# Two groups of pre-added weights, loaded at two moments instead of one

## The chip, the cores and the metric

The kernel runs on one core of a Trainium2 chip. The metric is the device time of one execution in microseconds (us). Three runs of the kernel before took 1237.09, 1238.32 and 1242.99 us; the median, 1238.32, is the time before.

## What is computed

The reference is a decoder trunk of two layers over 256 positions of width 1024, in float32:

```python
for l in range(DEPTH):                                   # DEPTH = 2
    x = x + 0.5 * swiglu_ffn(rms_norm(x, ffn1_norm[l]), ffn1_w_in[l], ffn1_w_out[l])
    h = rms_norm(x, mix_norm[l])
    uv, c_q, c_kv, k_rope, z, xbc, dt_raw, gates = split(h @ w_in[l])
    y_a, y_b, y_c = gmlp(uv), attention(c_q, c_kv, k_rope), ssd(z, xbc, dt_raw)
    g = sigmoid(gates)
    x = x + (sum_i g_i * (y_i @ w_branch[l, i])) @ w_out[l]
    x = x + 0.5 * swiglu_ffn(rms_norm(x, ffn2_norm[l]), ffn2_w_in[l], ffn2_w_out[l])

def swiglu_ffn(h, w_in, w_out):                          # w_in: 1024 x 5632, w_out: 2816 x 1024
    gate, up = split(h @ w_in, 2)
    return (silu(gate) * up) @ w_out
```

The change touches only the first product of `swiglu_ffn`, `h @ w_in`. It runs four times: FFN (0,0) and (0,1) in the first layer, (1,0) and (1,1) in the second, with the mixing part between the two of a layer.

## The kernel before

**Precision.** Each float32 matrix is cut into a high part (`whi`, a cast on ScalarE, L177) and a rest (`wlo`, a subtraction on VectorE, L178), and each product is three TensorE matmuls (L223 to L225): high x high, high x low, low x high.

**Weights.** All weights lie in one long array in the order of use, cut into chunks of 512 KB (128 x 1024). `load` (L147) brings a chunk into one of five `raw` buffers on SyncE's DMA queue; a load waits until the chunk five places earlier has been split. `split` cuts it into one of four pairs of `whi` and `wlo`, up to four chunks ahead of TensorE (`AHEAD = 3`, L130, L209).

**Narrow chunks.** 14 of the 22 blocks of 128 features come in seven narrow groups of four chunks. A narrow chunk is 12 matmuls, which fill `ps_in`.

**Wide groups.** The other 8 blocks come in two wide groups, j = 0 and 1. Each is a product of 2 x 2 blocks done with seven block products instead of eight, as in Winograd's form of Strassen's scheme. `b11`, `b22` and `b21` use blocks of the weight as they are; `t1` to `t4` use sums of blocks. Each of the seven steps is two chunks of six matmuls, as long in all as one narrow chunk. The results go to `ps_wa` (`wide["A"]`), `ps_wd` (`wide["D"]`) and `ps_we`. `wide["m"]` is a copy of A after b11 (L444); `wide["v"]` is a copy of A after t3, with D added.

**The sums.** t1's weight is b11 + b12 and t3's is b22 + b12. They are made by DMAs of the POOL (GpSimd) queue, in `load_sums` (L153): a plain load of the base chunk (L168), and on top of it an accumulating load of the b12 chunk (L171), which waits for the first. So each of t1 and t3 takes four transfers of 512 KB per group: two chunks, each loaded and then added to. The other sums are made on VectorE in place: t2 = t3 + b11 (L200; b11's chunk is loaded again for it), t4 = t2 + b21 (L195). In the code, b21's chunk is split and then added at L195.

**When the sums are loaded.** The first group's eight transfers are issued before the FFN starts, or in (0,0) once the norm's factors exist. The second group's eight are issued in program order after the step b22 of the first group. A DMA without a dependency may be moved up as far as its buffer is free. To hold t1's sums back, a POOL copy of one column from `wide["v"]` into their buffer stands ahead of them (`behind`, L165). t3's sums of both groups share one buffer (tag `xbc`) and have no copy for the second group; they start when the first group's t3 chunks have been read. t1's sums of the second group lie in a buffer of their own (tag `big12b`).

**Order.** The order of the chunks is `_ffn_order` (L55): `lead` narrow chunks, then the seven steps of group 0 with `gaps[0]` narrow chunks behind each, then group 1 with `gaps[1]`. Behind step b11 stands the place of b12, which takes no step. `aside`, the loads of the tables and of the mixing part's parameters, is called at entry 12 of the order in (0,0). The instruction order on each engine is then made by the Tile framework's planner, which runs the program through a timeline of its own; `split` is given high priority. Within an engine the instructions run in that order.

Of the kernel before, what the change touches and what calls it, by code (L numbers as in the profile page):

```python
# [10 lines left out]
F32 = mybir.dt.float32  # L11
# [4 lines left out]
ALU = mybir.AluOpType  # L16
# [3 lines left out]
P = 128  # L20
# [34 lines left out]
def _ffn_order(key):  # L55

    narrow = [("n", g, c) for g in range(NARROW) for c in range(4)]
    if key == (0, 0):
        lead, gaps = 12, [[2, 1, 1, 1, 1, 1, 1]] * 2
    else:  # L60
        lead, gaps = 4, [[2] * 7, [2, 1, 1, 2, 1, 1, 2]]
    order, narrow = narrow[:lead], narrow[lead:]
    for j in range(WIDE):
        for names, n in zip((("b11", "b12"), ("t1",), ("t2",), ("t3",), ("b22",), ("b21",), ("t4",)), gaps[j]):
            order += [(name, j, c) for name in names for c in range(2)]
            order += narrow[:n]
            narrow = narrow[n:]
    assert not narrow
    return order
# [36 lines left out]
SUB_MAX = 1024  # L106
# [4 lines left out]
def tile_trunk(ctx, tc, wst, xtok, xT, pos, pcol, prow, wsT, cst, out):  # L111
    nc = tc.nc
    act, dve, pool, pe = nc.scalar, nc.vector, nc.gpsimd, nc.tensor
# [3 lines left out]
    bp = ctx.enter_context(tc.tile_pool(name="bp", bufs=1))  # L117
# [5 lines left out]
    widths, units, chunk_at = _plan()  # L123
# [12 lines left out]
    def source(i):  # L136
        return wst[starts[i] : starts[i] + P * widths[i]].rearrange("(p n) -> p n", p=P)
# [12 lines left out]

    sums = {}

    def load_sums(key, j, behind=None):  # L153

        if j == 0:
            xs = [bp.tile([P, SUB_MAX], F32, name="xsum", tag=t) for t in ("vg", "zt")]
            sums[key, "y"] = bp.tile([P, 2, SUB_MAX], F32, name="ysum", tag="xbc")
        else:
            both = bp.tile([P, 2, SUB_MAX], F32, name="xsum", tag="big12b")
            xs = [both[:, c] for c in range(2)]  # L160
        for c in range(2):
            sums[key, "t1", j, c], sums[key, "t3", j, c] = xs[c], sums[key, "y"][:, c]
            if behind is not None:
                for t in (xs[c], sums[key, "y"][:, c])[: 2 - j]:
                    pool.tensor_copy(t[:, 0:1], behind)  # L165
        for name, base in (("t1", "b11"), ("t3", "b22")):
            for c in range(2):
                pool.dma_start(out=sums[key, name, j, c], in_=source(chunk_at[key, (base, j, c)]))  # L168
        for name in ("t1", "t3"):
            for c in range(2):  # L170
                pool.dma_start(out=sums[key, name, j, c], in_=source(chunk_at[key, ("b12", j, c)]), accum_op=ALU.add)  # L171

    def parts_of(r, cuts):
        hi = wp.tile([P, SUB_MAX], F32R, name="whi", tag="whi", bufs=4)
# [226 lines left out]
    def ffn(key, nrm, nxt, last, late, aside=None):  # L401
# [28 lines left out]
        def product(ps, xs, first):  # L430

            for c in range(2):
                hi, lo = next_sub()
                for i in range(2):
                    k, w = 2 * c + i, slice(512 * i, 512 * (i + 1))
                    xhi, xlo = xs(k)
                    mm3x(ps, xhi, xlo, hi[:, w], lo[:, w], first and k == 0, k == 3, again=not first)

        xs = {}
        wide = {}  # L440
# [12 lines left out]
        def wide_step(kind, j):  # L453
            if kind == "b11":
                wide["A"] = acc.tile([P, 512], F32, name="ps_wa", tag="acc")
                product(wide["A"], plain(0, 0), True)
                wide["m"] = snap("m1", "ss")
            elif kind == "t1":
                wide["D"] = acc.tile([P, 512], F32, name="ps_wd", tag="acc")
                product(wide["D"], summed(xs[0]), True)  # L460
            elif kind == "t2":
                product(wide["A"], summed(xs[2]), False)
                wide["u"] = snap("u2", "xp")
            elif kind == "t3":
                product(wide["A"], summed(xs[1]), False)
                wide["v"] = snap("u3", "xp")
                dve.tensor_tensor(wide["v"], wide["v"], wide["D"], ALU.add)
            elif kind == "b22":
                product(wide["D"], summed(xs[3]), False)
                dve.tensor_tensor(wide["u"], wide["u"], wide["D"], ALU.add)  # L470
            elif kind == "b21":
                e = mxp.tile([P, 512], F32, name="ps_we", tag="mx")
                product(e, plain(1, 0), True)
                dve.tensor_tensor(wide["m"], wide["m"], e, ALU.add)
                gated("a0", wide["m"], 0, wide["u"])
            else:
                product(wide["A"], plain(1, 1), False)
                gated("a1", wide["A"], 1, wide["v"])
                for n in range(2):
                    s = slice(256 * n, 256 * (n + 1))  # L480
                    turns.append((2 * NARROW + 4 * j + 2 * n, [wide["u"][:, s], wide["v"][:, s]]))

        ps = None
        for n, (kind, g, c) in enumerate(_ffn_order(key)):
            if n == 12 and aside:
                aside()
            if kind != "n":
                if kind != "b12" and c == 0:
                    wide_step(kind, g)
                    if kind == "b22" and g == 0:  # L490
                        load_sums(key, 1, wide["v"][:, 0:1])
                continue
            if c == 0:
                home, tag = (acc, "acc") if g % 2 == 0 else (mxp, "mx")
                ps = [home.tile([P, 512], F32, name="ps_in", tag=tag) for _ in range(2)]
            hi, lo = next_sub()
            for i in range(2):
                k, w = 2 * c + i, slice(512 * i, 512 * (i + 1))
                for b in range(2):
                    s = halves(b)  # L500
                    mm3x(ps[b], hl[:, k, 0, s], hl[:, k, 1, s], hi[:, w], lo[:, w], k == 0, k == KD - 1)
            if n < ready:
                late[n]()
            if n == ready - 1:
                nrm.finish()
                if key == (0, 0):
                    load_sums(key, 0, nrm.rc[:, 0:1])
                big = bp.tile([P, 3, 2, 4, P], F32R, name="xs", tag="big12a")
                spots = [(big[:, m, 0], big[:, m, 1]) for m in range(3)]
                spots.append([tp.tile([P, 4, P], F32R, name="xs", tag="prob") for _ in range(2)])  # L510
            elif n in (combine, combine + 1):
                for m in (0, 1) if n == combine else (2, 3):
                    xs[m] = combined(nrm, m, *spots[m])
            turn_all()
            if c == 3:
                aa = []
                for b in range(2):
                    rcb = nrm.rc[:, b : b + 1]
                    s = tp.tile([P, 256], F32, name="s", tag="s")
                    act.activation(s, ps[b][:, 0:256], AF.Silu, scale=rcb)  # L520
                    a = at[:, g % 2, b]
                    dve.scalar_tensor_tensor(a, ps[b][:, 256:512], rcb, s, ALU.mult, ALU.mult)
                    aa.append(a)
                turns.append((2 * g, aa))
        ahl = [parts[f // 12][:, f % 12] if parts[f // 12] is not None else None for f in range(KF)]

        for h in range(2):
            hs = slice(HD * h, HD * (h + 1))
            ps = [acc.tile([P, HD], F32, name="ps_out", tag="acc") for _ in range(2)]
            f = 0  # L530
            for c in range(KF // 2):
                hi, lo = next_sub()
                for i in range(2):
                    w = slice(512 * i, 512 * (i + 1))
                    for b in range(2):
                        s = halves(b)
                        mm3x(ps[b], ahl[f][:, 0, s], ahl[f][:, 1, s], hi[:, w], lo[:, w], f == 0, f == KF - 1)
                    f += 1
                if h == 0 and c == 0:
                    turn_all()  # L540
                if h == 1 and c == 0 and not last:
                    nxt.add(0)
                if h == 1 and c == 4 and key[1] == 1 and not last:
                    load_sums((key[0] + 1, 0), 0, None)
            for b in range(2):
                dve.scalar_tensor_tensor(x[:, b, hs], ps[b], FFN_RESID, x[:, b, hs], ALU.mult, ALU.add)
                if last:
                    nc.scalar.dma_start(out=out[:, b, hs], in_=x[:, b, hs])
# [576 lines left out]
    nrm = Norm(pc[:, 0, 0:8], "big24b")  # L1125
# [10 lines left out]
    for l in range(DEPTH):  # L1136
# [9 lines left out]
        nrm, nxt = nxt, Norm(pc[:, l, 16:24], "big24a")  # L1146
        late = mix(l, nrm, nxt, late, *params)
        nrm = nxt
# [3 lines left out]
        nrm = nxt  # L1152
# [117 lines left out]
```

## Time and profile before

| | |
|---|---|
| median of three runs | 1238.32 us |
| the profiled execution, its own time | 1240.04 us |
| its span, first to last instruction | 1238.2 us |
| TensorE (PE) busy | 1214.8 us, 98% |
| VectorE (DVE) busy | 897.2 us, 72% |
| ScalarE (ACT) busy | 736.0 us, 59% |
| GpSimd (POOL) busy | 113.6 us, 9% |
| mean granted TensorE clock | 0.996 |
| moved by DMA | 254.12 MB, mean 205 GB/s |

Line numbers (L178) are those of the kernel before. A row of the timeline gives the start in us, the duration, the engine and line, the operation with output and inputs, how many, and in brackets how long the engine was idle before it and what ended that. A row of the windows gives a stretch, its length, the busy time and the number of instructions of PE, PEld (weight load), DVE, ACT and POOL, then the granted clock, the DMA engines' mean busy share, and GB/s.

### The profile page before, as it was taken

The page shows a single profiled execution, that of the slowest core. Times are in us where ns is not written, and L with a number is a line of the kernel's source. Part 1 is how long each engine was busy: PE and PEld are TensorE (multiplying, and loading weights), DVE is VectorE, ACT ScalarE, POOL GpSimd, SP SyncE. Part 2 cuts the span into 40 slices and gives each one's busy share as a digit, 9 for nine tenths or more (in the row PEclk, how much of TensorE's full clock was granted, in tenths as well). Part 3 has the DMA queues.
Part 4 walks back from the last instruction along what each step waited for, and adds up shares of the span by engine and source line. Part 5 has one row for each costly group of instructions (what it writes and reads, how often), then busy time and mean ns, then how long its engine had stood idle before and what let it go on. Part 6 is the DMA issues. An engine that isn't in the chain of part 4 may idle for free.

```text
span 1238.2 us, 16875 instructions
## 1 busy us (share of the span) xinstructions
PE 1214.8 (98%) x6252; PEld 1024.2 (83%) x6252; DVE 897.2 (72%) x1249; ACT 736.0 (59%) x1009; POOL 113.6 (9%) x130
## 2 busy tenths in 40 slices
PE   9999999999999999999999999999998999999998
PEld 7887889999788877888887888899987887878886
DVE  6787756898757786885587885578795676877853
ACT  8565545756675475664575664457556755756632
POOL 3020000031300001000001000002131000010000
PEclk9999999999999999999999999999999999999999
DMA  9995554634547668976559755545454577596662
GB/s 345 288 294 199 188 187 157 208 125 171 181 152 229 213 204 260 325 245 214 187 165 275 249 192 191 189 151 188 128 160 145 180 227 235 183 270 219 226 192 72
DMA packets 72162, 254.12 MB, mean 205 GB/s; under 512 B 8080, under 2 KB 9360, under 8 KB 72080
## 3 DMA queue, kind: packets, MB, share of 16 engines
q1 hardware_dynamic: 61856, 218.29, 51.9%
q0 software_dynamic: 9216, 33.56, 11.0%
q10 hardware_dynamic: 1008, 1.20, 0.3%
q8 instruction: 49, 0.80, 0.3%
q14 instruction: 33, 0.27, 0.1%
HBM read 251.96 MB, written 1.05 MB: 204 GB/s over the span
## 4 chain that ended last, share of the span: by engine, by line
PE 83%; DMA 5%; DVE 5%; POOL 2%; issue 2%; ACT 2%; SPq 0%; DVEq 0%; ACTq 0%
PE ps_out L223 8%; PE ps_out L224 8%; PE ps_out L225 8%; PE ps_in L224 7%; PE ps_in L225 7%; PE ps_in L223 7%; DMA raw<-in_w 5%; PE ps_in L217 3%; PE ps_in L218 3%; PE ps_in L219 3%; DVE wlo L178 3%; PE ps_g L225 2%; PE ps_g L224 2%; PE ps_g L223 2%; PE ps_br L225 2%; PE ps_wa L224 2%
## 5 line engine op out<-in xcount | busy, mean ns | idle before, releaser
L178 DVE TENSOR_TENSOR wlo<-raw,whi 128x1024 fp32r<-128x1024 f32 (+3 forms) x401 | 483.6, 1210 | 215.0 <-ACT whi L177 212.7
L177 ACT CAST whi<-raw 128x1024 fp32r<-128x1024 f32 (+3 forms) x401 | 415.6, 1039 | 347.4 <-PE ps_out L225 131.3
L224 PE MATMUL ps_in<-wlo,xg 128*128 128x512 f32 x448 | 176.2, 394 | 7.8 <-DVE wlo L178 7.8
L225 PE MATMUL ps_in<-whi,xg 128*128 128x512 f32 x448 | 173.9, 394 | 0.1
L223 PE MATMUL ps_in<-whi,xg 128*128 128x512 f32 x448 | 163.8, 398 | 1.2 <-ACT xg L331 1.2
L224 PEld LDWEIGHTS ps_in<-wlo,xg 128*128 128x128 f32 x448 | 84.4, 188 | 27.4 <-DVE wlo L178 9.9
L225 PEld LDWEIGHTS ps_in<-whi,xg 128*128 128x128 f32 x448 | 83.9, 189 | 17.3 <-DVE xg L332 0.5
L223 PEld LDWEIGHTS ps_in<-whi,xg 128*128 128x128 f32 x448 | 83.0, 189 | 17.9 <-ACT xg L331 1.6
L218 PE MATMUL ps_in<-xg,whi 128*128 128x256 f32 x336 | 95.4, 286 | 0.0
L219 PE MATMUL ps_in<-xg,wlo 128*128 128x256 f32 x336 | 94.5, 283 | 0.0
L217 PE MATMUL ps_in<-xg,whi 128*128 128x256 f32 x336 | 94.5, 287 | 0.0
L224 PE MATMUL ps_g<-wlo,xg 128*128 128x512 f32 x192 | 76.7, 400 | 0.0
L225 PE MATMUL ps_g<-whi,xg 128*128 128x512 f32 x192 | 76.7, 399 | 0.0
L224 PE MATMUL ps_out<-wlo,aa 128*128 128x512 f32 x192 | 75.8, 395 | 0.0
L225 PE MATMUL ps_out<-whi,aa 128*128 128x512 f32 x192 | 75.4, 393 | 0.0
L223 PE MATMUL ps_out<-whi,aa 128*128 128x512 f32 x192 | 75.1, 392 | 0.0
L223 PE MATMUL ps_g<-whi,xg 128*128 128x512 f32 x192 | 74.5, 398 | 0.0
L219 PEld LDWEIGHTS ps_in<-xg,wlo 128*128 128x128 f32 x336 | 64.0, 191 | 0.3
L218 PEld LDWEIGHTS ps_in<-xg,whi 128*128 128x128 f32 x336 | 64.0, 191 | 0.1
L217 PEld LDWEIGHTS ps_in<-xg,whi 128*128 128x128 f32 x336 | 63.1, 190 | 1.0 <-issue 0.7
L224 PE MATMUL ps_out<-wlo,ab 128*128 128x512 f32 x160 | 62.2, 389 | 0.0
L223 PE MATMUL ps_out<-whi,ab 128*128 128x512 f32 x160 | 62.2, 389 | 0.0
(328 smaller groups left out, 2362.9 us busy)
## 6 DMA issues: line engine op xcount, KB each, us to landing
raw<-in_w SPq DMA_DIRECT2D x397, 512.0 KB, 4.2
xsum<-in_w POOLq DMA_DIRECT2D x32, 512.0 KB, 8.7
ysum<-in_w POOLq DMA_DIRECT2D x32, 512.0 KB, 8.4
raw<-in_w SPq DMA_DIRECT2D x8, 414.0 KB, 3.6
raw<-in_w SPq DMA_DIRECT2D x6, 384.0 KB, 3.0
raw<-in_w SPq DMA_DIRECT2D x4, 276.0 KB, 3.0
x<-in_x SPq DMA_DIRECT2D x4, 256.0 KB, 5.6
out_x<-x ACTq DMA_DIRECT2D x4, 256.0 KB, 3.8
```

The source lines that it names most:

```text
L177: act.copy(hi[:, a:b], r[:, a:b])
L178: dve.tensor_tensor(lo[:, a:b], r[:, a:b], hi[:, a:b].bitcast(F32), ALU.subtract)
L217: pe.matmul(ps, lhsT=whi, rhs=xhl[:, 0], start=first, stop=False)
L218: pe.matmul(ps, lhsT=whi, rhs=xhl[:, 1], start=False, stop=False)
L219: pe.matmul(ps, lhsT=wlo, rhs=xhl[:, 0], start=False, stop=last)
L223: pe.matmul(ps, lhsT=xhi, rhs=whi, start=first, stop=False, skip_group_check=again)
L224: pe.matmul(ps, lhsT=xhi, rhs=wlo, start=False, stop=False, skip_group_check=again)
L225: pe.matmul(ps, lhsT=xlo, rhs=whi, start=False, stop=last, skip_group_check=again)
```

## The change

The sums of the second wide group are no longer loaded in one go. `load_sums` takes the names of the sums as an argument. t1's four transfers of group 1 are called at group 0's b11, behind a copy from `wide["m"]`; t3's four are called at group 0's b22, behind copies from `wide["v"]`. t3's buffer becomes a tile of its own for each group, with the same tag. The call for the first group keeps both names.

The narrow chunks are placed anew in group 0. In (0,0) `lead` falls from 12 to 10, group 0 gets 11 narrow chunks instead of 8 and group 1 seven instead of eight. In the other three FFNs group 0 keeps 14: behind b11, t1, t2, t3, b22, b21, t4 there stood two each, and now 2, 1, 2, 2, 3, 3, 1.

```diff
     if key == (0, 0):
-        lead, gaps = 12, [[2, 1, 1, 1, 1, 1, 1]] * 2
+        lead, gaps = 10, [[2, 1, 1, 2, 2, 2, 1], [1] * 7]
     else:
-        lead, gaps = 4, [[2] * 7, [2, 1, 1, 2, 1, 1, 2]]
+        lead, gaps = 4, [[2, 1, 2, 2, 3, 3, 1], [2, 1, 1, 2, 1, 1, 2]]
...
-    def load_sums(key, j, behind=None):
-
-        if j == 0:
-            xs = [bp.tile([P, SUB_MAX], F32, name="xsum", tag=t) for t in ("vg", "zt")]
-            sums[key, "y"] = bp.tile([P, 2, SUB_MAX], F32, name="ysum", tag="xbc")
-        else:
-            both = bp.tile([P, 2, SUB_MAX], F32, name="xsum", tag="big12b")
-            xs = [both[:, c] for c in range(2)]
-        for c in range(2):
-            sums[key, "t1", j, c], sums[key, "t3", j, c] = xs[c], sums[key, "y"][:, c]
-            if behind is not None:
-                for t in (xs[c], sums[key, "y"][:, c])[: 2 - j]:
-                    pool.tensor_copy(t[:, 0:1], behind)
-        for name, base in (("t1", "b11"), ("t3", "b22")):
-            for c in range(2):
-                pool.dma_start(out=sums[key, name, j, c], in_=source(chunk_at[key, (base, j, c)]))
-        for name in ("t1", "t3"):
-            for c in range(2):
-                pool.dma_start(out=sums[key, name, j, c], in_=source(chunk_at[key, ("b12", j, c)]), accum_op=ALU.add)
+    def load_sums(key, j, names=("t1", "t3"), behind=None):
+
+
+        for name in names:
+            if name == "t3":
+                y = bp.tile([P, 2, SUB_MAX], F32, name="ysum", tag="xbc")
+                ts = [y[:, c] for c in range(2)]
+            elif j == 0:
+                ts = [bp.tile([P, SUB_MAX], F32, name="xsum", tag=t) for t in ("vg", "zt")]
+            else:
+                both = bp.tile([P, 2, SUB_MAX], F32, name="xsum", tag="big12b")
+                ts = [both[:, c] for c in range(2)]
+            for c in range(2):
+                sums[key, name, j, c] = ts[c]
+                if behind is not None:
+                    pool.tensor_copy(ts[c][:, 0:1], behind)
+        for base in (0, 1):
+            for name in names:
+                for c in range(2):
+                    if base == 0:
+                        b = "b11" if name == "t1" else "b22"
+                        pool.dma_start(out=sums[key, name, j, c], in_=source(chunk_at[key, (b, j, c)]))
+                    else:
+                        pool.dma_start(
+                            out=sums[key, name, j, c], in_=source(chunk_at[key, ("b12", j, c)]), accum_op=ALU.add
+                        )
...
                     wide_step(kind, g)
+                    if kind == "b11" and g == 0:
+                        load_sums(key, 1, ("t1",), wide["m"][:, 0:1])
                     if kind == "b22" and g == 0:
-                        load_sums(key, 1, wide["v"][:, 0:1])
+                        load_sums(key, 1, ("t3",), wide["v"][:, 0:1])
...
                 if key == (0, 0):
-                    load_sums(key, 0, nrm.rc[:, 0:1])
+                    load_sums(key, 0, behind=nrm.rc[:, 0:1])
```

More of the change, by code (lines that the diff above doesn't have):

```diff
@@ L543, in ffn @@
                 if h == 1 and c == 4 and key[1] == 1 and not last:
-                    load_sums((key[0] + 1, 0), 0, None)
+                    load_sums((key[0] + 1, 0), 0)
             for b in range(2):
```

## The prediction

> **What bounds the kernel now.** I read the page's busy times first, then what TensorE waited for over the whole run, then the same question for a stretch around each FFN. Columns of a wait: total us, times, longest.
>
> ```profile
> PE 1214.8 (98%) x6252; PEld 1024.2 (83%) x6252; DVE 897.2 (72%) x1249; ACT 736.0 (59%) x1009; POOL 113.6 (9%) x130
> PE ps_in L224 <- DVE wlo L178: 7.8, 4, 2.3
> PE ps_t L976 <- DVE qk L940: 3.8, 2, 3.1
> PE ps_wa L224 <- DVE wlo L178: 1.6, 2, 1.1
> PE ps_in L224 <- DVE wlo L178: 2.1, 1, 2.1
> PE ps_in L224 <- DVE wlo L178: 2.3, 1, 2.3
> PE ps_in L224 <- DVE wlo L178: 1.7, 1, 1.7
> ```
>
> TensorE is the bound. It is idle 1238.2 - 1214.8 = 23.4 us, and no edit of order can win more than that. The last three rows are FFN (0,1), (1,0) and (1,1): each has one wait of about 2 us on a `wlo`. The fourth, again 1.7, is in (0,0). The changed loop can touch the first and third waits (9.4 us); the 3.1 us in attention (L976) it doesn't touch.
>
> The wait in (0,1), by the timelines of ScalarE, VectorE and TensorE:
>
> ```profile
> 483.76 1.05 ACT L177 CAST whi<-raw 128x1024 fp32r<-128x1024 f32 x1 [0.21 <-PE ps_in L225]
> 487.03 1.23 DVE L195 TENSOR_TENSOR xsum<-xsum,raw 128x1024 f32<-128x1024 f32 x1 [3.69 <-DMA raw<-in_w]
> 489.74 1.23 DVE L195 TENSOR_TENSOR xsum<-xsum,raw 128x1024 f32<-128x1024 f32 x1 [1.09 <-DMA raw<-in_w]
> 490.88 1.22 DVE L178 TENSOR_TENSOR wlo<-raw,whi 128x1024 fp32r<-128x1024 f32 x1
> 492.16 0.51 PE L224 MATMUL ps_in<-wlo,xg 128*128 128x512 f32 x1 [2.08 <-DVE wlo L178]
> ```
>
> The narrow chunk that TensorE lacks was cast at 483.76 and could have had its `wlo` at 484.8. But VectorE works in order, and two adds of the b21 chunks (L195) stand ahead. They wait for their raw loads until 487.0 and 489.7. So a late raw of b21 stops a narrow chunk that has long been there. Why the raw is late, by the POOL timeline and by the raw loads issued in three stretches (437 to 470, 470 to 477, 477 to 482):
>
> ```profile
> 471.29 0.59 POOL L168 DMA_DIRECT2D ysum<-in_w  x1 [29.57 <-DVE wlo L178]
> 477.47 0.87 POOL L171 DMA_DIRECT2D ysum<-in_w  x1 [0.72 <-DMA ysum<-in_w]
> 481.36 0.30 POOL L165 COPY xsum<-u 128x1 f32<-128x1 f32 x2 [3.02 <-DVE u L467]
> 481.87 1.11 POOL L168 DMA_DIRECT2D xsum<-in_w  x2 [0.22 <-POOL xsum L165]
> DMA to landing us min/median/max: 3.1/3.3/5.2
> DMA to landing us min/median/max: 6.5/6.5/6.5
> L147 SPq DMA_DIRECT2D raw<-in_w x3: 328/328/328, 477.9 to 480.7; - x3
> DMA to landing us min/median/max: 9.1/10.4/11.5
> ```
>
> All eight sum transfers of the second group run from 471 on: t3's (`ysum`) first, as soon as their buffer is free, then t1's (`xsum`), held until `wide["v"]` exists. A raw needs 3.3 us when POOL is silent, 6.5 us as it starts, 10.4 us in the thick of it.
>
> **The change, part by part.** A sum transfer's weight, from the page's queues:
>
> ```profile
> q1 hardware_dynamic: 61856, 218.29, 51.9%
> q0 software_dynamic: 9216, 33.56, 11.0%
> ```
>
> 33.56 MB are 64 transfers of 0.524 MB: 0.110 x 1238.2 / 64 = 2.1 us of all 16 engines each; a raw is 0.519 x 1238.2 / 416 = 1.5 us. Four sums are 8.5 us.
>
> *t1's four sums move to b11.* Their gate becomes `wide["m"]`, copied here:
>
> ```profile
> 455.24 0.59 ACT L444 COPY m<-ps_wa 128x512 f32<-128x512 f32 x1
> 457.00:462.00 5.00, 5.00 (x26) 4.05 (x25) 5.00 (x5) 2.95 (x5) 0.00 (x0) 1.00 0.41 124
> 482.00:487.00 5.00, 5.00 (x23) 4.10 (x22) 1.22 (x1) 1.98 (x4) 0.98 (x2) 1.00 1.04 283
> ```
>
> The last but one column is the DMA share: 0.41 just after `m`, 1.04 at the wait. The 8.5 us go from a full stretch into one with room, and raws read just after `m` were issued before it, because a load goes out when the chunk five back is split. Cost here nothing. With that cover gone, the first raw issued after `m` (about 459.8) is for the narrow chunk behind t3, which TensorE reaches near 475; less cast and `wlo` (2.3) it would have to take 13 us to be missed, longer than any landing quoted here.
>
> *t3's four move from 471.3 to about 481.9*, behind the copies that wait for `v`. So 471 to 482 gets free of POOL transfers, and 482 onward holds four instead of the last two of t3 and four of t1.
>
> *Three narrow chunks instead of two before b21* (and three after). A narrow chunk is 12 matmuls at 0.23 us (row below), 2.76 us. With one more ahead, the b21 raws take the second and third of the three issues above (about 479.3 and 480.7) instead of the first two, still ahead of POOL's 481.87. The chunk behind the second add is needed 2.76 us later than the wait's start at 490.1, at 492.8. After the raw lands come the add (1.23), an L522 (0.48) and a `wlo` (1.22): 2.9. So the wait returns only if a raw takes longer than 492.8 - 480.7 - 2.9 = 9.2 us. Between the ends 3.3 and 11.5 I take 6.5, the row with POOL just starting. The three waits go: **-6.1** (bounds 0, at 11.5, to -6.1). Two more POOL copies per FFN, 0.15 us each, lie in POOL's 91% idle time; uncovered they cost 0.3 per FFN.
>
> *FFN (0,0).* Here lead falls from 12 to 10, so b11 comes two narrow chunks sooner, into a stretch full of DMA. Rows: six windows (DMA share last but one, granted clock before it), then a TensorE wait at b11, raw landings for 30 to 40 us, two POOL issues, a piece of the chain of waits, an add and a split of the second group, and two matmuls of the chain:
>
> ```profile
> 35.00:40.00 5.00, 5.00 (x25) 4.09 (x25) 2.58 (x4) 1.73 (x3) 0.00 (x0) 1.00 1.05 277
> 50.00:55.00 5.00, 5.00 (x24) 4.14 (x23) 5.00 (x6) 2.72 (x4) 0.00 (x0) 1.00 0.76 271
> 55.00:60.00 5.00, 5.00 (x24) 4.14 (x23) 3.85 (x4) 2.76 (x4) 0.00 (x0) 1.00 0.69 244
> 60.00:65.00 5.00, 5.00 (x24) 4.14 (x23) 4.48 (x4) 3.91 (x6) 1.10 (x2) 1.00 0.54 193
> 115.00:120.00 5.00, 3.08 (x14) 1.96 (x13) 4.50 (x5) 1.53 (x2) 0.00 (x0) 0.93 0.76 256
> 120.00:125.00 5.00, 5.00 (x18) 3.99 (x17) 2.11 (x3) 1.86 (x2) 0.00 (x0) 0.73 0.59 203
> 46.40 0.50 PE L224 MATMUL ps_wa<-wlo,xg 128*128 128x512 f32 x1 [0.49 <-DVE wlo L178]
> DMA to landing us min/median/max: 10.1/11.0/12.1
> 73.64 1.10 POOL L168 DMA_DIRECT2D xsum<-in_w  x2 [0.18 <-POOL xsum L165]
> 84.75 0.87 POOL L171 DMA_DIRECT2D xsum<-in_w  x1 [2.45 <-DMA xsum<-in_w]
> 86.27 9.21 DMA raw<-in_w
> 109.14 1.23 DVE L195 TENSOR_TENSOR xsum<-xsum,raw 128x1024 f32<-128x1024 f32 x1 [3.45 <-DMA raw<-in_w]
> 110.29 1.22 DVE L178 TENSOR_TENSOR wlo<-ysum,whi 128x1024 fp32r<-128x1024 f32 x1
> 119.11 0.23 PE ps_in L225
> 120.52 0.43 PE ps_in L224
> ```
>
> The fourteenth raw is late by 0.49 us today, for the second half of b11. After the change it is read by the second narrow chunk behind b11, which starts half a unit (1.4 us) sooner: **+1.4** (bounds 0 to +2.8, one whole unit). The parameter loads now fall behind b11 in program order; nothing gates them, so I leave them where they run and cost them at nothing; late, they would take two raws' time (about 1 MB, 3 us) inside these bounds' stretch.
>
> In the second group the chain runs from the raw at 86.27 (9.21 us, POOL's last sums beside it) through VectorE's splits to the b21 add at 109.14, with t3's `wlo` behind it, and ends in waits of 1.1 and 1.7; the granted clock then falls to 0.93 and 0.73: 5 x 0.07 + 5 x 0.27 = 1.7 us (a matmul takes 0.43 instead of 0.23). Together 4.5. After the change only t3's sums are left there, and `v` comes two chunks sooner (about 5.5 less the 1.4 above, 68 to 69 instead of 73), so that raw can land some 4 us sooner. The row of splits behind it stays, with one narrow chunk fewer between b11 and t1 to hide it. Between all and nothing I take half: **-2.2** (bounds 0 to -4.5).
>
> TensorE: Matmul & The Clock Gate of the Trainium skill (section Why this matters for your kernels) says the clock drops after idle gaps above about 3 us. Here the longest single wait was 1.7, so the rule by itself would price no dip; by it the sum below would lose half the dip, 0.85, and be -6.0. The trace's 0.73 decides.
>
> **Sum:** -6.1 + 1.4 - 2.2 = -6.9. The profiled execution took 1240.04 (span 1238.2, 1.84 around it), so it would take 1233.1 and a span of 1231.3. The median of the runs, 1238.32, lies 1.7 below its own time: 1231.4.
>
> **The rivals.**
> 1. *The raws stay late.* Four sums still start next to b21. At 10.4 us the wait is 1.2 each: 1238.3 - 6.1 + 3.6 + 1.4 - 2.2 = 1235.0. For it: 10.4 is the median beside POOL; against: then six transfers were in flight, now four. DMA: Bandwidth & Descriptors of the Trainium skill (Queues, rings and completion order) says that each engine takes turns between queues; by that raws near b21 still get every other turn, and the rise from 3.3 to 10.4 agrees.
> 2. *Slower: (0,0) runs out of transfers.* t1's 8.5 us move from 73 to 42. Up to t3 there are two raws fewer (3.1 us) in 5.5 us less time: 8.5 - 3.1 + 5.5 = 10.9 us more wanted, while 50 to 65 has 5 x (0.24 + 0.31 + 0.46) = 5.0 to spare. The shortfall is 5.9, and so long a wait brings the 1.7 of clock again, with no win in group two: -6.1 + 5.9 + 1.4 + 1.7 = +2.9, 1241.2. It decides from a shortfall of 6.1 - 1.4 - 1.7 = 3.0 on. Against: sums are not urgent there, and raws at half rate (3.0 us each) about meet the need of six in seven units (3.2 us each).
> 3. *It doesn't do it.* The planner orders VectorE by its own times; it may again put both adds ahead of a chunk needed sooner, or lose elsewhere, as L976's 3.1 against 0.7 in the two layers shows. About 1238.
> 4. *All of it.* Terms at their good ends: -6.1 - 0.5 - 4.5 = -11.1, 1227.2.
>
> **How the numbers follow.** Forecast 0.52 (its own range 1228.5 to 1234.5), raws late 0.18, slower 0.12, nothing 0.10, all 0.08. The range goes from 1226.0 (1227.2 less the 1.2 by which the lowest run is below the median) to 1239.5; the worst ends of the terms (0, +2.8, 0) give 1241.1, cut since rival 2 beyond it holds under 0.1. A measurement tells about 0.5%, 6.2 us: below 1232.1 is faster. That holds 0.78 of the forecast, all of case 4, a tenth of case 1: 0.50. Slower needs above 1244.5: a third of case 2 and a little of 3: 0.05. The rest, 0.45, is the same.
>
> **What would show it.** No `ps_in` wait on `wlo` near b21 in (0,1), (1,0), (1,1), and no idle of 3.69 and 1.09 ahead of the L195 adds; raws issued before b21 landing under 9.2 us; `xsum` issues right after `m`, `ysum` after `v`; DMA share above 0.7 after `m`. A b11 wait of about 1.9 us in (0,0), and a clock of 1.00 at 115 to 125. Wrong would be: b21 waits as long as before, a new wait behind L200, or longer idle at L976.

## The result, and the profile after

The changed kernel took **1231.3 us** in the median (1226.9 to 1234.1, six runs), the kernel before 1237.4 beside it (1233.3 to 1243.0, six runs). The ratio is 0.9944, 95% interval [0.9923, 0.9965]: 6.9 us won by the ratio, with an interval of 4.3 to 9.5 (the two medians differ by 6.1). Forecast were 1231.4 and 6.9 us. The size was right; which parts of the change earn it was not, as the experiments show.

The profiled execution took 1231.88 us, span 1230.0. Of the 8.2 us of span won, 3.2 are idle time of TensorE (23.4 before, 20.2 now) and 5.0 are busy time. The page's busy times, then what TensorE waited for: three rows of the whole run, then the stretches around the second group of (0,0), and around b21 in (0,1), (1,0) and (1,1). Columns of a wait: total us, times, longest. Line numbers are now those of the kernel that the rows come from; in the changed one L185 makes `wlo`, L202 is the b21 add, L168 the copy that holds a sum back, L174 and L176 its two loads.

```profile
PE 1209.8 (98%) x6252; PEld 1021.0 (83%) x6252; DVE 896.7 (73%) x1249; ACT 735.5 (60%) x1009; POOL 128.2 (10%) x138
PE ps_in L231 <- DVE wlo L185: 4.4, 4, 2.4
PE ps_t L985 <- DVE qk L949: 3.8, 2, 3.1
PE ps_x L352 <- DMA x<-in_x: 2.4, 1, 2.4
PE ps_in L231 <- DVE wlo L185: 0.7, 1, 0.7
PE ps_we L230 <- ACT whi L184: 0.2, 1, 0.2
PE ps_in L231 <- DVE wlo L185: 0.7, 1, 0.7
PE ps_in L231 <- DVE wlo L185: 0.7, 1, 0.7
PE ps_in L231 <- DVE wlo L185: 2.4, 1, 2.4
```

The waits in (0,0)'s second group fell from 3.06 us (1.68 + 1.15 + 0.23) to 0.95 (0.70 + 0.25). The three b21 waits were 2.1 + 2.3 + 1.7 = 6.1 and are 0.7 + 0.7 + 2.4 = 3.8: smaller, not gone, and the last is longer than it was in this profile (0.7 in a second one, below). The load of `x` at the start cost 1.4 us more in this execution (1.0 before), which the change doesn't touch.

Most of the busy time is clock. The same windows, before (the first) and after (the rest); the last but two column is the granted clock:

```profile
935.00:940.00 5.00, 5.00 (x18) 3.94 (x16) 3.70 (x4) 2.42 (x4) 0.00 (x0) 0.66 0.54 182
```

```profile
935.00:940.00 5.00, 5.00 (x27) 4.26 (x26) 2.83 (x9) 3.87 (x9) 0.00 (x0) 1.00 0.82 297
115.00:120.00 5.00, 4.29 (x20) 3.50 (x20) 3.59 (x5) 1.33 (x2) 0.00 (x0) 1.00 0.79 260
120.00:125.00 5.00, 5.00 (x23) 4.12 (x22) 4.83 (x6) 3.92 (x4) 0.00 (x0) 1.00 0.69 222
```

Two dips of the clock are gone, each worth 1.7 us, 3.4 of the 5.0 (the rest was not traced): the one in (0,0) behind the shortened waits (5 x 0.07 + 5 x 0.27), and one behind the 3.1 us attention wait (5 x 0.34), although that wait is as long as before. So a part of 8.2 is this execution's luck.

Why a b21 wait is left in (0,1): VectorE, TensorE and POOL of the changed kernel.

```profile
477.70 1.23 DVE L202 TENSOR_TENSOR xsum<-xsum,raw 128x1024 f32<-128x1024 f32 x1 [3.59 <-DMA raw<-in_w]
478.84 1.22 DVE L185 TENSOR_TENSOR wlo<-raw,whi 128x1024 fp32r<-128x1024 f32 x1
479.97 1.22 DVE L202 TENSOR_TENSOR xsum<-xsum,raw 128x1024 f32<-128x1024 f32 x1
480.11 0.50 PE L231 MATMUL ps_in<-wlo,xg 128*128 128x512 f32 x1 [0.66 <-DVE wlo L185]
451.09 6.38 POOL L168 COPY xsum<-m 128x1 f32<-128x1 f32 x2 [14.19 <-ACT m L451]
457.65 1.17 POOL L174 DMA_DIRECT2D xsum<-in_w  x2 [0.18 <-POOL xsum L168]
464.78 0.88 POOL L176 DMA_DIRECT2D xsum<-in_w  x1 [0.40 <-DMA xsum<-in_w]
473.37 0.30 POOL L168 COPY ysum<-u 128x1 f32<-128x1 f32 x2 [7.71 <-DVE u L474]
473.86 1.09 POOL L174 DMA_DIRECT2D ysum<-in_w  x2 [0.18 <-POOL ysum L168]
```

The planner now puts one add ahead of the narrow chunk's `wlo`, not two, and VectorE still idles 3.59 us ahead of that add for b21's raw. And the two one-column copies that hold t1's sums back took 6.38 us together, where the same two copies take 0.30 for t3's. So t1's first transfers begin at 457.7, where the gate was open at 451.1.

### The profile page after: what moved, and what is told of

Read it like the earlier page. It is cut to its first block, busy times and chain, and to the rows that moved or that the text cites. A ratio compares the mean times of both kernels' runs of the same rounds, so it can differ in the third digit from the quotient of the medians.

```text
span 1230.0 us, 16889 instructions
## 1 busy us (share of the span) xinstructions
PE 1209.8 (98%) x6252; PEld 1021.0 (83%) x6252; DVE 896.7 (73%) x1249; ACT 735.5 (60%) x1009; POOL 128.2 (10%) x138
## 3 DMA queue, kind: packets, MB, share of 16 engines
HBM read 251.96 MB, written 1.05 MB: 206 GB/s over the span
## 4 chain that ended last, share of the span: by engine, by line
PE 84%; DVE 5%; DMA 5%; ACT 2%; issue 2%; POOL 2%; SPq 0%; ACTq 0%; DVEq 0%
PE ps_out L230 8%; PE ps_out L232 8%; PE ps_out L231 8%; PE ps_in L231 7%; PE ps_in L232 7%; PE ps_in L230 6%; DMA raw<-in_w 4%; PE ps_in L224 3%; PE ps_in L225 3%; PE ps_in L226 3%; PE ps_g L232 2%; PE ps_g L231 2%; PE ps_g L230 2%; DVE wlo L185 2%; PE ps_wa L230 2%; PE ps_wa L232 2%
## 5 line engine op out<-in xcount | busy, mean ns | idle before, releaser
L185 DVE TENSOR_TENSOR wlo<-raw,whi 128x1024 fp32r<-128x1024 f32 (+3 forms) x401 | 483.8, 1211 | 216.3 <-ACT whi L184 214.2
```

The lines of the kernel that those rows point to most:

```text
L185: dve.tensor_tensor(lo[:, a:b], r[:, a:b], hi[:, a:b].bitcast(F32), ALU.subtract)
```

## The experiments

Two theories stood at the start: the loads earn the gain, or the places do; and each could do so in (0,0) or in the other three FFNs.

**Loads alone.** The changed `load_sums` and its calls, with the old places in all four FFNs:

```
-        lead, gaps = 10, [[2, 1, 1, 2, 2, 2, 1], [1] * 7]
+        lead, gaps = 12, [[2, 1, 1, 1, 1, 1, 1]] * 2
     else:
-        lead, gaps = 4, [[2, 1, 2, 2, 3, 3, 1], [2, 1, 1, 2, 1, 1, 2]]
+        lead, gaps = 4, [[2] * 7, [2, 1, 1, 2, 1, 1, 2]]
```

> The two loads of sums at b11 and b22 as in the change, the narrow chunks in their old places. Theory A (what pays is that POOL's transfers are spread): the raws of b21 in FFN (0,1), (1,0), (1,1) land in 4 to 8 us instead of 9 to 11, their waits of 2.1, 2.3 and 1.7 fall below 1 each, and in (0,0) the second group's waits of 1.1 and 1.7 with the clock dip of 1.7 mostly go: 4 to 8 us faster. Theory B (the new places pay, the spread alone only shifts which sums stand beside b21): within 2 us of before.

Measured: 1231.5 us, ratio 0.9928 [0.9904, 0.9952]. No b21 wait is left in any of the three. In (0,1), its raw loads issued from 476 to 482, its VectorE at b21, and POOL:

```profile
L147 SPq DMA_DIRECT2D raw<-in_w x3: 327/328/328, 477.7 to 480.4; - x3
DMA to landing us min/median/max: 5.1/5.1/5.1
482.84 1.23 DVE L202 TENSOR_TENSOR xsum<-xsum,raw 128x1024 f32<-128x1024 f32 x1 [1.86 <-DMA raw<-in_w]
483.98 1.22 DVE L185 TENSOR_TENSOR wlo<-raw,whi 128x1024 fp32r<-128x1024 f32 x1
455.65 7.52 POOL L168 COPY xsum<-m 128x1 f32<-128x1 f32 x2 [14.19 <-ACT m L451]
481.05 0.30 POOL L168 COPY ysum<-u 128x1 f32<-128x1 f32 x2 [9.53 <-DVE u L474]
```

For comparison, the changed kernel's raws issued from 470 to 476:

```profile
L147 SPq DMA_DIRECT2D raw<-in_w x3: 328/328/328, 469.9 to 472.7; - x3
DMA to landing us min/median/max: 6.4/6.5/7.2
```

The new places have one narrow chunk fewer between t1 and t2, so the gate `v` of t3's sums opens 22.3 us behind `m`'s (451.1 to 473.4), not 25.4 (455.7 to 481.1). t3's sums then start 4.3 us ahead of the first b21 add (473.4 to 477.7) instead of 1.8, and the raws take 6.4 to 7.2 us instead of 5.1. The forecast had the third narrow chunk as the reason why the waits go. Without it they go altogether.

In (0,0) the loads alone take away the two long waits of the second group (0.23 of 3.06 us is left), and a new one comes at b21 of the first group, with the raws issued from 56 to 62:

```profile
74.33 0.50 PE L231 MATMUL ps_in<-wlo,xg 128*128 128x512 f32 x1 [1.54 <-DVE wlo L185]
L147 SPq DMA_DIRECT2D raw<-in_w x2: 328/328/328, 56.4 to 60.0; - x2
DMA to landing us min/median/max: 9.4/9.5/9.7
```

t1's sums of the second group run there now: their first transfers are issued at 52.4, their last at 60.6. So the wait has moved from the second group to the first. With the new places b21 of the first group stands two narrow chunks further behind b11, and it has no such wait.

**Places alone.** The kernel before with the new lead and gaps.

> The narrow chunks in the new places, all eight sums in one go after b22 as before. Theory A: the raws near b21 still land in 9 to 11 us, the waits fall only by what the third narrow chunk covers (about 2.7 less one later place in the queue), 0 to 3 us faster. Theory B: 4 to 8 us faster, with the waits near b21 below 1 us.

Measured: 1238.5 us, ratio 0.9984 [0.9965, 1.0002], no difference that could be told. b21 waits of 2.6, 0.6 and 2.1 us; (0,0)'s second group has only 0.42 + 0.24. VectorE in (0,1), its raws issued from 466 to 476, and two windows of clock:

```profile
L147 SPq DMA_DIRECT2D raw<-in_w x5: 327/328/452, 467.5 to 475.7; - x5
DMA to landing us min/median/max: 6.6/10.8/12.2
482.25 1.23 DVE L195 TENSOR_TENSOR xsum<-xsum,raw 128x1024 f32<-128x1024 f32 x1 [6.62 <-DMA raw<-in_w]
483.40 1.22 DVE L178 TENSOR_TENSOR wlo<-raw,whi 128x1024 fp32r<-128x1024 f32 x1
480.00:490.00 10.00, 7.38 (x25) 5.60 (x25) 7.63 (x8) 4.28 (x6) 1.74 (x2) 0.83 0.96 297
1090.00:1100.00 10.00, 7.91 (x29) 6.03 (x28) 6.48 (x7) 3.56 (x6) 1.76 (x2) 0.83 0.98 324
```

Here the `wlo` also stands behind one add only, and the wait is there, because the raws land late. So one add ahead is no cure when the landing takes 10.8 us. The waits by part, from one profile of each kernel, in us:

| | (0,0), first group | (0,0), second group | b21 in the other three |
|---|---|---|---|
| before | 0.7 | 3.1 | 6.1 |
| loads alone | 2.3 | 0.2 | 0 |
| places alone | 0.2 | 0.7 | 5.3 |
| both (the change) | 0.2 | 1.0 | 3.8 |

In (0,0)'s second group either half takes the long waits away; in the first group the loads need the places. In the other three the loads take the waits away, and the places bring some back. The other profiles agree on these three: with the old loads (before, places alone, (0,0) alone) nine of nine b21s wait, 0.6 to 2.6 us; with the new loads in the old places (loads alone and two runs below) none of nine; with the new loads in the new places (the change, its repeat, the other three alone) eight of nine, 0.3 to 2.4 us, together 3.8, 1.8 and 2.4 in the three profiles.

**The change in (0,0) alone, and in the other three alone**, with the kernel before elsewhere (`load_both` is the old `load_sums`):

```
+                    if key == (0, 0):        # the other run: key != (0, 0)
                         if kind == "b11" and g == 0:
                             load_sums(key, 1, ("t1",), wide["m"][:, 0:1])
                         if kind == "b22" and g == 0:
                             load_sums(key, 1, ("t3",), wide["v"][:, 0:1])
+                    elif kind == "b22" and g == 0:
+                        load_both(key, 1, wide["v"][:, 0:1])
```

> Loads and places changed in FFN (0,0) alone. By the profile after, most of the gain lies there: the second group's waits went from 1.1 + 1.7 to 0.7 + 0.2, the clock dip of 1.7 behind them is gone, b11's 0.5 is 0.2. Expected 3 to 5 us faster. If instead the three other FFNs carry it, under 2 us.

> Loads and places changed in FFN (0,1), (1,0), (1,1), not in (0,0). By the profile after their waits near b21 went from 2.1 + 2.3 + 1.7 = 6.1 to about 1.2 + 0.7 + 2.4 = 4.3: 1 to 3 us faster. By the prediction's first term, 6 us faster. Together with the run that changes (0,0) alone it should give the change's 6 to 8.

Measured: (0,0) alone 1232.9 us in the median of five executions (a sixth took 5268.0 us and is left out), 0.9940 [0.9916, 0.9964]; the others alone 1237.1 us, 0.9982 [0.9965, 1.0000]. In microseconds -7.4 [-10.4, -4.5] and -2.2 [-4.3, 0]. Their sum, -9.6, is larger than the whole; the intervals hold both. So most of the change's gain is in (0,0), and in the other three it earns little.

**The gate copied on ScalarE.** Theory A: a one-column copy on POOL can't run while VectorE works without a gap, so t1's sums start late and run into t3's. Rival: the places alone make the raws late. VectorE's order is the same as in the change.

```
-                    pool.tensor_copy(ts[c][:, 0:1], behind)
+                    (act.copy if j else pool.tensor_copy)(ts[c][:, 0:1], behind)
```

> The changed kernel, with the one-column copies that hold the second group's sums back made by ScalarE instead of POOL; VectorE's order is the same. In the profile after the two copies behind m took 6.4 us in FFN (0,1) and (1,1), 2.4 in (1,0), 0.3 in (0,0), while VectorE ran without a gap. Theory A (VectorE's work holds POOL's copy up, so t1's sums run late into the stretch of t3's): the copies take under 1 us, t1's transfers start 6 us sooner, raws of b21 land in under 6 us, the waits of 0.7, 0.7 and 2.4 near b21 fall to under 1 in all: 2 to 4 us faster than the changed kernel. Theory B (t3's sums alone delay those raws): the waits stay within 0.5 each.

Measured: 1229.9 us, 0.9923 [0.9902, 0.9944]. No b21 wait is left in any of the three. Two short waits on `wlo` stand elsewhere, 17 us and more behind the first b21 add of their FFN (476.96 in (0,1), 659.49 in (1,0)):

```profile
517.97 0.50 PE L231 MATMUL ps_in<-wlo,xg 128*128 128x512 f32 x1 [0.41 <-DVE wlo L185]
677.12 0.50 PE L231 MATMUL ps_in<-wlo,xg 128*128 128x512 f32 x1 [0.53 <-DVE wlo L185]
451.94 0.30 ACT L168 COPY xsum<-m 128x1 f32<-128x1 f32 x2
452.45 1.15 POOL L174 DMA_DIRECT2D xsum<-in_w  x2 [15.06 <-ACT xsum L168]
458.12 0.88 POOL L176 DMA_DIRECT2D xsum<-in_w  x1 [0.35 <-DMA xsum<-in_w]
```

The copies take 0.30 us, and t1's last transfer is issued 6.7 us sooner than in the change (458.1, not 464.8). The b21 raws of (0,1), issued from 470 to 476, take 5.0 to 5.2 us instead of 6.4 to 7.2. The waits go with it, none of three where the same order with copies on POOL has eight of nine: theory A holds for the waits. That the time falls too can't be told from this run: its interval overlaps the change's.

**t3's sums begun at b21** instead of at b22, behind `u`:

```
-                    if kind == "b22" and g == 0:
-                        load_sums(key, 1, ("t3",), wide["v"][:, 0:1])
+                    if kind == "b21" and g == 0:
+                        load_sums(key, 1, ("t3",), wide["u"][:, 0:1])
```

> The changed kernel with t3's sums of the second group called after b21 instead of after b22, behind a copy from the finished first half. Theory B (t3's sums delay b21's raws): these land in 3 to 5 us and the waits of 0.7, 0.7 and 2.4 near b21 are gone. Theory A (t1's late sums): they stay above half. Either way a new wait may come where t2 of the second group needs t3's sums: up to 3 us in each FFN if four transfers in 20 us are too late.

Measured: 1236.5 us (1232.0 to 1240.6, ten runs), 0.9975 [0.9959, 0.9991]. No b21 wait on `wlo` is left in the three, so t3's sums beside b21 are a condition of the wait as much as t1's late ones. Yet the time is hardly better than before. The profiled execution (1232.0) is the fastest of the ten, so its trace doesn't show what the others lose. They take 5.1 us more in the mean, and their mean granted clock is 0.9957 against its 0.997: an estimate of 0.0013 x 1235 = 1.6 us for the clock. The rest stays open.

**No adds at b21**, in the kernel before; t4's product is then taken with t2's weight:

```
-                if kind == "b21":
-                    dve.tensor_tensor(t, t, r, ALU.add)
```

> The kernel before, leaving out the sixteen adds of b21 to t4's weight on VectorE (so t4's product is taken with t2's weight); every load stays. Theory A (a narrow chunk's rest stands in VectorE's queue behind an add that waits for its raw): raws still land in 9 to 11 us there, but the waits of 2.1, 2.3 and 1.7 in the three FFNs are below 0.5 each, and 1.1 + 1.7 in (0,0) mostly gone: 5 to 10 us faster with the clock dips. Theory B (TensorE simply lacks the late b21 chunk itself): the waits move to b21's own product and stay at 1.5 or more each.

Measured: 1229.2 us, 0.9923 [0.9900, 0.9947]. The waits in the three FFNs are gone although the raws are about as late as before (issued from 474 to 484; 6.5, 10.4 and 11.5 there before):

```profile
DMA to landing us min/median/max: 8.5/9.7/10.9
```

So in these FFNs a late raw stops TensorE only through the add that waits for it at the head of VectorE's queue, as the forecast read it. (The adds' own 1.23 us each go too; a VectorE that idles 3.69 us for a raw doesn't lack them.) In (0,0)'s second group the waits at 111.6 and 118.6 are gone, and two others of 1.0 and 0.8 us come at 101.6 and 103.3, of which the first is on another VectorE result (`ab`); why is open.

**New places in (0,0) only, changed loads everywhere:**

```
-        lead, gaps = 4, [[2, 1, 2, 2, 3, 3, 1], [2, 1, 1, 2, 1, 1, 2]]
+        lead, gaps = 4, [[2] * 7, [2, 1, 1, 2, 1, 1, 2]]
```

> The sums loaded as in the change everywhere; the narrow chunks in the new places only in FFN (0,0), in the old ones in the other three. From the runs so far: no waits near b21 in the three (as with the loads alone), 0.2 + 0.2 in (0,0) (as with the first FFN alone): 2 to 3 us below the loads alone, 9 to 12 us faster than before, ratio 0.990 to 0.993. If the new places in the three FFNs do pay, it is no faster than the change, 0.994.

Measured: 1228.6 us (1226.9 to 1232.6), 0.9920 [0.9899, 0.9941]. (0,0)'s second group waits 0.39 + 0.25, b21 in the other three not at all. By the time it can't be told from the loads alone (0.9928).

**The same with the copies on ScalarE, and the changed kernel once more**, on one chip:

> The changed loads in all four FFNs, the new narrow places in FFN (0,0) alone, and the one-column gate copies of the second group on ScalarE. Theory A (POOL's copy, held 6 to 7.5 us while VectorE works without a gap, costs time only where t1's sums then run into t3's ahead of b21): with the old places in the other three FFNs no b21 wait was left, so there is nothing to win; ratio as with the copies on POOL, 0.990 to 0.994, copies about 0.3 us. Rival (the held-up copies, or the POOL transfers that start late behind them, cost more than the b21 waits show): 1 to 3 us below, ratio 0.988 to 0.990.

> The changed kernel itself, on the chip of the run beside it. If its difference from the kernel before is what the first measurement said, the ratio is 0.992 to 0.9965, time about 1232. Theory A: it stands 2 to 3 us above the run with the new places in (0,0) alone, which is the sum of the b21 waits that are left in it (0.7, 0.7 and 2.4 us in its profile, less what an execution without a clock dip gets back). Rival (the places of the three other FFNs cost nothing that can be measured): both within 1 us.

Measured: 1230.2 us, 0.9916 [0.9901, 0.9932], and 1233.2 us, 0.9948 [0.9926, 0.9970], with 1239.6 before. The change repeats its first ratio to 0.0004. Beside it the version with old places in three FFNs and the gate on ScalarE is 3.0 us lower, as its lack of b21 waits (0 against 1.1 + 0.7 in this profile of the change) would have it, with some left over. The two ratios' intervals overlap by 0.0006. The executions compared directly, six against nine, differ by 3.1 us in the mean, 95% interval 0.8 to 5.3 (of which the granted clocks, 0.9973 and 0.9969, make an estimated 0.5). So the old places in the three are very likely better, though this pair differs in the gate as well. Copies on ScalarE add nothing that can be told to the old places (0.9916 and 0.9920), where POOL's copy takes 7.53 us and no wait follows: here a late gate costs only where its transfers run into the next ones.

## Why the prediction was right or wrong

**The bound and the mechanism: right.** TensorE was the bound, and what moved were single waits of it on `wlo`. The adds of b21 at the head of VectorE's queue made them: without the adds they are gone at raw landings of 8.5 to 10.9 us.

**Term A, -6.1 for the three b21 waits: mis-sized.** In the two profiles of the change 3.8 and 1.8 us are left of 6.1, in that of the other three alone 2.4, so 2.3 to 4.3 were won. The step that failed is "with one more ahead, the b21 raws take the second and third of the three issues", with a narrow chunk that stands "behind the second add" and is needed at 492.8. It kept the old timetable and moved one chunk in it. But the new places take a chunk away between t1 and t2, so `v`, and t3's sums behind it, come sooner against b21, and the planner puts the narrow `wlo` behind the first add (with the loads alone too). The slack against which 6.5 us was weighed did not exist: the raws did take 6.4 to 7.2, far below the 9.2 of the forecast, and the wait came all the same. With the loads alone all 6.1 go.

**Copies at 0.15 us each in idle POOL: wrong by a factor of twenty.** Two took 6.38 us in (0,1), 6.39 in (1,1), 2.36 in (1,0), and 0.30 in (0,0). "Uncovered 0.3 per FFN" used the row of two copies at 481.36, a moment at which VectorE was waiting. The cost is not POOL's time but the late start of t1's sums; with the copies on ScalarE the waits of 0.7, 0.7 and 2.4 are gone.

**t1's sums moved to `m`, at nothing: wrong beside the new places, and in (0,0) beside the old ones** (the new wait of 1.54 with the loads alone). With the copies held, the windows of the changed kernel from 462 on are full:

```profile
457.00:462.00 5.00, 5.00 (x24) 4.13 (x23) 4.41 (x6) 3.31 (x4) 1.64 (x4) 1.00 0.80 288
462.00:467.00 5.00, 5.00 (x24) 4.14 (x23) 3.44 (x4) 3.43 (x5) 1.76 (x2) 1.00 1.05 355
467.00:472.00 5.00, 5.00 (x24) 4.11 (x23) 3.97 (x5) 3.65 (x4) 0.00 (x0) 1.00 1.01 220
472.00:477.00 5.00, 5.00 (x25) 4.07 (x25) 2.00 (x3) 2.40 (x3) 1.39 (x4) 1.00 1.01 370
```

The DMA share (last but one) reaches 1.01 to 1.05 until t3's sums begin, where the forecast had 0.41 and room.

**Term B, +1.4 at b11 of (0,0): wrong in sign, and outside its bounds of 0 to +2.8.** The wait of 0.49 there is gone; one of 0.2 on a cast stands in front of another product (45.58), and in the second profile of the change none. The step said "the fourteenth raw is late". The rows of ScalarE before don't show that:

```profile
43.68 0.47 ACT L520 ACTIVATE s<-ps_in,rs_x 128x256 f32<-128x256 f32 x1 [2.83 <-PE ps_in L225]
44.05 1.04 ACT L177 CAST whi<-raw 128x1024 fp32r<-128x1024 f32 x1
45.12 1.22 DVE L178 TENSOR_TENSOR wlo<-raw,whi 128x1024 fp32r<-128x1024 f32 x1 [0.45 <-ACT whi L177]
```

The cast stood behind an activation that waited 2.83 us for TensorE to end a narrow block, and followed it at once. With b11 two chunks sooner, that block ends elsewhere. I took a wait on `wlo` for a wait on a transfer without following it one engine further.

**Term C, -2.2 in the second group of (0,0): inside its bounds, by a reason that is half of it.** Its waits fell by 2.1, and the dip of 1.7 behind them was gone in both profiles of the change (together 3.8). The forecast gave this to t1's sums, moved out of the way, and with the loads alone the two waits do go (0.2 of 3.1 is left). But with the places alone they go too (0.7 is left), which the term didn't foresee; and what it left out is the first group, where the loads without the places add 1.5. The dip is not sure to follow those waits, so its absence is in part luck: in the run with the change in the other three alone (0,0)'s second group still waited 2.6 us in all, and the clock stayed at 1.00:

```profile
115.00:120.00 5.00, 2.96 (x14) 1.91 (x14) 4.38 (x6) 2.16 (x4) 0.00 (x0) 1.00 0.84 280
120.00:125.00 5.00, 5.00 (x22) 4.04 (x22) 3.40 (x5) 2.10 (x2) 0.00 (x0) 1.00 0.69 229
```

**The sum** came out by luck: term A was too good, and B and C too poor by about as much. By the runs of each half (0,0) earns 7.4 and the other three 2.2, where the terms had 0.8 and 6.1. Of (0,0)'s 7.4 the waits explain 3.3 in the profile of that run (0.45 us instead of 3.78, b11's included). The mean granted clock of its five executions, 0.9974 against 0.9960 before, makes an estimate of 0.0014 x 1238 = 1.7 more. That sum, 5.0, lies inside the interval (from 4.5); whether the change brought that clock wasn't tested.

**Rivals.** Neither the slower one ((0,0) out of transfers) nor "it doesn't do it" occurred: (0,0) is where it won. The first, raws that stay late, happened in a milder form: they took 6.4 to 7.2 us and not 10.4, and were still late for the add. Every other turn for a raw, as that rival has it, would by itself make about 6.6 us of 3.3 (an estimate), so the 10.4 agree with it in direction only. The fourth, all of it at 1227.2, didn't occur either.

## What to carry to other kernels

Cost a step that is moved together with all that its gate moves: whoever shortens the way to a gate starts the transfers behind it sooner, and they may land on the load that the move was to free. Follow a wait one engine further back before naming a transfer as its cause, since an in-order queue can hold a chunk that has long been there. And test the two halves of a change in each place apart: here, by the waits, the loads in three FFNs are good, the places in these three are not, and in the fourth the loads need the places; the sum hid it.

## What was unexpected in the hardware

**A one-column copy on POOL can take microseconds.** Two took 6.36 to 7.53 us in (0,1) and (1,1) in each of the six profiles that have them there behind `m`, and 0.30 where VectorE idled or ran an operation that reads PSUM. VectorE in the changed kernel during the 6.38 us, first and last of its gap-free row:

```profile
450.95 1.21 DVE L185 TENSOR_TENSOR wlo<-xsum,whi 128x1024 fp32r<-128x1024 f32 x1
456.10 1.21 DVE L185 TENSOR_TENSOR wlo<-xsum,whi 128x1024 fp32r<-128x1024 f32 x1
457.23 0.68 DVE L405 TENSOR_TENSOR aa<-ps_a,aa 128x512 fp32r<-128x512 f32 x1
```

From 450.95 to 457.23 it runs six operations of two SBUF operands each; the copies end at 457.47, just as one that reads PSUM (`ps_a`) comes. Two shorter holds end the same way: 2.36 us in (1,0), at 640.04, with an operation on `ps_in` begun at 639.80; and 2.25 us in the second profile, at 67.81, with one begun at 67.68. The Trainium skill, SBUF — State Buffer (section SBUF: two separate sides), says that VectorE with two SBUF inputs and a POOL operation that reads SBUF lock each other out, each for a whole instruction. The trace agrees, and goes further: the copy was held over a row of operations, not over one of 1.2 us. No run here changed VectorE's operands, so that this lock is the cause is argued; shown is that on ScalarE they take 0.30.

**The clock dips behind short waits, and not behind each.** In the run of the places alone the clock fell to 0.83 over 10 us (1.7 us lost) around single waits of 2.6 and 2.1 us. In the kernel before, the 2.1 us wait at 490 had none:

```profile
490.00:495.00 5.00, 2.92 (x15) 2.36 (x15) 5.00 (x6) 2.15 (x3) 1.74 (x2) 1.00 0.91 244
```

and the 3.1 us attention wait had one in nine of the twelve profiles and none in three, the first of the change among them. The Trainium skill, TensorE: Matmul & The Clock Gate (section Why this matters for your kernels), puts the bound at idle gaps above about 3 us. Here dips came below it, and not always above it, so a single execution carries a luck of about 1.7 us for each such wait. In the 23 executions of the kernel before beside the first experiments, which spread by 9.1 us, 0.001 less of mean granted clock goes with 1.3 us more (correlation -0.75). Not all of the spread is clock: the wait for `x` at the start is 0.8 to 2.8 us in the profiles, the attention wait of the first layer 0.4 to 2.7.
